# A transformer block's attention: probabilities transposed in quarters of 32 rows instead of halves of 64

## The chip, the cores and the metric

The kernel runs on one core of one Trainium2 chip. The metric is the device time of one execution in microseconds. Before the change it was 1009.75 us, the median of three runs (1009.56 to 1010.26).

## The reference

One layer of a diffusion backbone on 1024 latent tokens and 256 context tokens of width 1024, all in 32-bit floats. Half of the mixing width is a pooling mixer, half is neighbourhood attention with 8 heads of 64 on a latent grid of 16 rows by 64 columns; then come an output projection and a squared-ReLU MLP. The change lies in the attention. Cut to what matters:

```python
s_loc = einsum('bnqhd,brnkhd->bhnqrk', q_r, k_b) * scale       # 8 x 16 window
s_loc = where(col_mask, s_loc + bias, -inf)                    # learned 2-D bias
s_ctx = einsum('bnqhd,bkhd->bhnqk', q_r, k_ctx) * scale        # all context keys
p = softmax(concatenate([s_loc, s_ctx]), axis=-1)
o = einsum(p_loc, v_b) + einsum(p_ctx, v_ctx)
```

## The kernel before, in words

Whole kernel: a startup stage (modulation, norms, transposes of the tokens), the projections, the attention, the output projection and the MLP. All products are TensorE matmuls on 32-bit data, most of them on a split into a high and a low part. TensorE is busy nearly all the time.

The attention works through 32 *units* (`units`, L1232), a pair of heads `j` (0 to 3) by a tile `m` (0 to 7) of 128 queries, 16 grid rows by 8 columns. The two heads of a pair lie on partitions 0 to 63 and 64 to 127. An *inner* unit (m from 1 to 6) has 384 local keys and 256 context keys, 640 in all; a unit at the edge of the grid has 512. Each unit goes through these steps:

- `scores` (L1255): products of queries and keys for each of the heads e = 0, 1 into a pair of PSUM banks S. Weights are 64 rows (the head's features) by 128 queries; the two heads run side by side in the two halves of the array.
- `biased` (L1275): VectorE adds the table of bias and mask, writes the rows `sp` to SBUF and the row's extreme `nm`.
- `exps` (L1286): ScalarE takes the exponential in place and sums each row. `share` (L1290, L1292) makes the reciprocals of the sums and spreads them over `rb` of 128x128, on GpSimd.
- `turn` (L1298 to L1317): TensorE transposes the probabilities, so that the keys lie on the partitions. A transpose is a matmul with the block of probabilities as the weights and a piece of the identity as the streamed data. A block of 128 queries by 128 keys is turned in two halves of 64 queries, one in each half of the array, each into a bank of its own. The *side blocks* go to the columns of the banks `pa` and `pz`: the reciprocals, and for an inner unit the fifth block of keys of each head. The eight *main blocks* (four by two heads) go to the two banks `T_0` and `T_1`, 512 columns each.
- `fifth_kept` (L1322): ScalarE copies the side blocks to SBUF (`px`), a copy for each bank. `turn_kept` (L1327): ScalarE copies T_0 and VectorE T_1 into the page `pt`, 128x512 each.
- `values` (L1342): the value sums, 16 or 20 matmuls with weights of 128 keys by 64 features, the two heads in the two column halves of the array, into one of two places in `pa`, by turns.
- `weighed` (L1352): VectorE multiplies the sum with the turned reciprocals into the page `f`.

The loop over units (`for i in range(N)`) interleaves them by hand. In round i stand, in this order, `weighed(i-4)`, `scores(i)`, `biased(i)`, then what else the round has to do for other stages (`jobs`, loads, sums by DMA), `turn(i-2)`, its side copies, `exps(i, 0)`, the first copy of the turn, `exps(i, 1)`, the second copy, and `values(i-3)`. Each engine's queue keeps this order. Both T banks, and pa and pz, are there once: the turn of a round waits until the copies of the round before are done. The last two units (N-2 and N-1) are turned after the loop, between the first sums of the output projection; the last of them goes to a tile of its own, `Tlate`.

pa and pz also serve, in round 2, three small column sums (`mod_gate`, `column_sums`, matmuls at L264).

Of the kernel before, what the change touches and what calls it, by code (L numbers as in the profile page):

```python
# [11 lines left out]
F32 = mybir.dt.float32  # L12
# [6 lines left out]
P = 128  # L19
# [7 lines left out]
HD = 64  # L27
# [8 lines left out]
NM = GW // QC  # L36
# [72 lines left out]
def hybrid_block(ctx, tc, x, ctx_in, w_mod, mod_pages, w_u, b_mod, gp1, gp2, w_in, pool_w, rpb, w_out, w1, w2, vectors,  # L109
                 mask, edge, out):  # L110
    nc = tc.nc
# [15 lines left out]
    def page(name, dt=F32):  # L127
        return act.tile([P, 1024], dt, tag="pg", name=name)
# [21 lines left out]
    ident = cst("ident", [P, P])  # L150
# [123 lines left out]
    def mod_gate(name, acc, g, bank):  # L274
        nc.vector.tensor_tensor(acc[:, :256], mod_sums_of(name, acc, bank), g, mul)
# [23 lines left out]
    with tc.tile_pool(name="ps1", bufs=6, space=PSUM) as ps1, tc.tile_pool(name="tmp1", bufs=3) as tmp:  # L299

        def bank(name):
            if name[:2] == "pm" or name in ("pxt5", "pxb2", "pxb3", "pxb4", "pxb5", "pcs", "pcr"):
                return lasting(name)
            return ps1.tile([P, 512], F32, tag="mm", name=name)
# [9 lines left out]
        cols = cst("cols", [P, 56])  # L314
# [195 lines left out]
        whole, pt = {}, {}  # L510
# [320 lines left out]
        accs = {}  # L831
# [14 lines left out]
        def column_sums(name, acc, bank):  # L846
            nc.scalar.copy(acc[:, :256], mod_sums_of(name, acc, bank))
# [332 lines left out]
        with in_order(ET.PE, ET.Pool, ET.Activation, ET.DVE, ET.SP) as pooling:  # L1180
            banks = {of: [bank(f"p{of}{j}") for j in range(2)] for of in "KQ"}
            use(-1)
            for step, (n, of, j) in enumerate([(n, of, j) for n, of in products for j in range(2)]):
                half_product(n, of, j, banks[of])
                use(step)
                if step in (5, 9, 17):
                    name = {5: "S1", 9: "S4", 17: "S3"}[step]
# [4 lines left out]
                if step in (7, 11):  # L1192
                    name = {7: "S4", 11: "S3"}[step]
# [32 lines left out]
    with (  # L1226
# [9 lines left out]
        both_sides = {None: (pa[:, 256:448], pz[:, :192])}  # L1236


        def scores(i):
            j, m = units[i]  # L1240
# [54 lines left out]

        def turn(i, t=None, more=None):  # L1298
            inner = 0 < units[i][1] < NM - 1
            if t is None:  # L1300
                t = [bank(f"T{i}_{h}") for h in range(2)]
            sides = both_sides[i] = more or both_sides[None]
            turned[i] = t
            halves = [slice(h * HD, (h + 1) * HD) for h in range(2)]

            def both(to, src):
                for h, hs in enumerate(halves):
                    nc.tensor.transpose(to(h), src(hs), ident[hs, hs])  # L1308
# [9 lines left out]
        def fifth_kept(i):  # L1318
            n = (3 if 0 < units[i][1] < NM - 1 else 1) * HD
            fifths[i] = att.tile([P, 384], F32, tag="px", name=f"px{i}", bufs=4).rearrange("p (h t) -> p h t", h=2)  # L1320
            for h in range(2):
                nc.scalar.copy(fifths[i][:, h, :n], both_sides[i][h][:, :n])  # L1322

        def turn_kept(i, h, copy):
            if h == 0:
                turns[i] = page(f"pt{i}").rearrange("p (e i t) -> p e i t", e=2, i=4)
            copy(turns[i].rearrange("p e i t -> p (e i) t")[:, :, h * HD : (h + 1) * HD],  # L1327
                 turned[i][h].rearrange("p (a t) -> p a t", a=8))

        def values(i):  # L1330
            j, m = units[i]
            vc = [vcp[:, 0:512], vcp[:, 512:1024]]
            if 0 < m < NM - 1:
                vs = vb[m - 1 : m + 2] + vc
            else:
                o = 1 if m == 0 else 0
                vs = vc + vb[m + o - 1 : m + o + 1]
            cols = slice((i % 2) * P, (i % 2 + 1) * P)
            for c, v in enumerate(vs):
                for e in range(2):  # L1340
                    f = (2 * j + e) * HD
                    nc.tensor.matmul(pa[e * HD : (e + 1) * HD, cols], v[:, f : f + HD],  # L1342
                                     turns[i][:, e, c] if c < 4 else fifths[i][:, :, (e + 1) * HD : (e + 2) * HD],
                                     start=(c == 0), stop=(c == len(vs) - 1))


        def weighed(i):
            j, m = units[i]
            if m == 0:
                heads[j] = page(f"f{j}")  # L1350
            to = heads[j].rearrange("p (m h t) -> p m h t", h=2, t=HD)[:, m, ::-1, ::-1]
            nc.vector.tensor_tensor(to, pa[:, (i % 2) * P : (i % 2 + 1) * P].rearrange("p (h t) -> p h t", h=2),  # L1352
                                    fifths[i][:, :, :HD], mul)

        N = len(units)
# [88 lines left out]
        with in_order(ET.PE, ET.Activation, ET.DVE, ET.SP) as projected:  # L1444
# [16 lines left out]
            def right_added(j):  # L1461
# [16 lines left out]
            rest_of_bank = lambda name: pz[:, 256:]  # L1478
            for i in range(N):
                if i in LOADS:  # L1480
                    weight_load(0, kks[LOADS.index(i)])
                if i == N - 2:
                    G1 = gate_page("a")
                if i > 3:
                    weighed(i - 4)
                if i == 0:
                    gain = mod_gain(gp1, att.tile([P, 256], F32, tag="gp", name="gpa"), nc.sync)
                    accs["sh"] = page("accsh2")
                    nc.sync.dma_start(accs["sh"], kept_row)
                if i == 2:  # L1490
                    mod_gate("a", accs["a"], gain, rest_of_bank)
# [12 lines left out]
                for f, *args in jobs.get(i, ()):  # L1504
                    f(*args)
                if block_copies and (i < 4 or 6 < i):
                    block_copied()
                for _ in range(SUMS.count(i)):
                    block_summed()
                if i == 2:  # L1510
                    late_query = part_page("qP0_1", False)
                    qparts[0, 1] = late_query[:, :512], late_query[:, 512:]
                    high_part(qT[0][1], qparts[0, 1][0])
                if i > 1:
                    turn(i - 2)
                    fifth_kept(i - 2)
                if i == 2:
                    turn_kept(0, 0, nc.scalar.copy)
                    column_sums("sc", accs["sc"], lambda name: pa[:, :256])
                if i == N - 1:  # L1520
                    turn_kept(i - 2, 0, nc.scalar.copy)
                    turn_kept(i - 2, 1, nc.vector.tensor_copy)
                    biased(i, 1)
                exps(i, 0)
                if i == 2:
                    column_sums("sh", accs["sh"], rest_of_bank)
                if 2 < i < N - 1:
                    turn_kept(i - 2, 0, nc.scalar.copy)
                exps(i, 1)
                if i == 0:  # L1530
                    key_parts(2, 0, True, "lo")
                    key_parts(2, 1, True, "lo")
                    query_parts(2, 0, False, "lo")
                if 1 < i < N - 1:
                    turn_kept(i - 2, 1, nc.vector.tensor_copy)
# [30 lines left out]
            weighed(N - 3)  # L1566
            low()
            turn(N - 2)
            fifth_kept(N - 2)
            first_sums_kept(0)  # L1570
            late = ps_s.tile([P, 1024], F32, tag="S", name="Tlate")
            turn(N - 1, [late[:, :512], late[:, 512:]], (pa[:, 448:], pz[:, 448:]))
            turn_kept(N - 2, 0, nc.scalar.copy)
            turn_kept(N - 2, 1, nc.vector.tensor_copy)
            fifth_kept(N - 1)
            turn_kept(N - 1, 0, nc.scalar.copy)
            turn_kept(N - 1, 1, nc.vector.tensor_copy)
            weight_split(5)
            weight_split(6)
            first_sums(1)  # L1580
# [950 lines left out]
```

## Time and profile before

| | |
|---|---|
| median of three runs | 1009.75 us |
| the profiled execution's own time | 1010.35 us |
| its span, first to last instruction | 1008.6 us |
| granted TensorE clock | 0.998 of full speed |
| transposes of turns into T | 225.0 to 316.7 us of the span |
| TensorE busy from 255 to 270 us | 15.00 of 15.00 us |
| VectorE, ScalarE, GpSimd in the same stretch | 12.04, 13.54, 14.83 us |

The trace gives each instruction's start and duration. In the lists a group reads: line, engine, operation, tile written and tiles read, rows by columns of the array for a matmul, shape, count. PE stands for TensorE's matmuls, PEld for its weight loads, DVE for VectorE, ACT for ScalarE, POOL for GpSimd. A weight load of the next matmul can run while a matmul streams. Since a matmul's record includes its way through the array, records of successive ones overlap; the cost of one in a row of them is the distance between starts. In a timeline, successive equal instructions are merged to one row with the start of the first, the time to the end of the last, and their count.

### The profile page before, as it was taken

What the parts mean: (1) busy time and instruction counts of PE and PEld (TensorE: products, weight loads), DVE (VectorE), ACT (ScalarE), POOL (GpSimd) and SP (SyncE); (2) the same over time, 40 slices, a digit from 0 to 9 for tenths busy, and PEclk for the clock granted to TensorE, in tenths of its full rate; (3) what the DMA queues carried; (4) which work ended last, traced back from release to release, by engine and by line L of the source; (5) the groups of instructions that cost most, each with busy time, mean ns of one, the idle gap of its engine ahead of it and who ended that gap; (6) DMA issues with size and microseconds to landing.
All of it is one profiled execution on the core that took longest, in us unless ns stands there. A gap on an engine that the chain in (4) does not pass through costs nothing.

```text
span 1008.6 us, 16695 instructions
## 1 busy us (share of the span) xinstructions
PE 997.9 (99%) x6062; PEld 829.4 (82%) x6062; DVE 798.6 (79%) x1276; ACT 581.0 (58%) x1038; POOL 201.9 (20%) x278
## 2 busy tenths in 40 slices
PE   8999999999999999999999999999999999999997
PEld 5788888878998888888888888888888888888886
DVE  5589766968885689879998888754798888888895
ACT  6673254448886746786555544545556565544551
POOL 4111110166985232410000000000001000021121
PEclk9999999999999999999999999999999999999999
DMA  9999798665989979986776666625999999579944
GB/s 362 396 278 340 237 273 306 219 160 194 230 184 249 238 191 274 297 208 205 261 252 217 201 215 221 213 89 184 333 371 300 286 341 322 171 220 315 318 166 162
DMA packets 146882, 252.10 MB, mean 250 GB/s; under 512 B 10417, under 2 KB 76849, under 8 KB 146801
## 3 DMA queue, kind: packets, MB, share of 16 engines
q1 hardware_dynamic: 111024, 181.63, 52.9%
q0 software_dynamic: 18640, 38.45, 19.8%
q10 hardware_dynamic: 17136, 30.97, 8.3%
q8 instruction: 47, 0.77, 0.3%
q14 instruction: 35, 0.28, 0.1%
HBM read 197.52 MB, written 69.22 MB: 264 GB/s over the span
## 4 chain that ended last, share of the span: by engine, by line
PE 96%; DVE 1%; DMA 1%; ACT 1%; issue 0%; POOL 0%; SPq 0%; DVEq 0%; POOLq 0%; ACTq 0%
PE pu L481 5%; PE pyiM L2394 4%; PE pyiN L2394 4%; PE pa L1342 4%; PE S L1255 3%; PE phx L226 3%; PE phz L226 3%; PE phv L226 3%; PE pyx L226 3%; PE pyx L227 3%; PE pyx L228 3%; PE phx L228 3%; PE phz L228 3%; PE phv L228 3%; PE phx L227 3%; PE phv L227 3%
## 5 line engine op out<-in xcount | busy, mean ns | idle before, releaser
L1962 ACT ACTIVATE c<-c 128x512 f32<-128x512 f32 x48 | 30.3, 631 | 44.2 <-DVE c L2084 25.3
L174 ACT CAST wpS<-S 128x512 fp32r<-128x512 f32 x64 | 38.7, 617 | 28.6 <-PE phv L228 10.1
L1286 ACT ACTIVATE sp<-sp,nm 128x640 f32<-128x640 f32 (+1 forms) x64 | 51.4, 804 | 6.1 <-DVE ri L1290 5.0
L1275 DVE CUSTOM_DVE_ANT_0 sp<-S,tab 128x640 f32<-128x640 f32 (+1 forms) x56 | 44.5, 795 | 13.0 <-PE pz L1308 9.8
L226 PE MATMUL phx<-thB,wpA 128*128 128x512 f32 x128 | 50.2, 392 | 0.0
L180 DVE TENSOR_TENSOR wpS<-S,wpS 128x512 fp32r<-128x512 f32 x64 | 43.4, 686 | 8.2 <-ACT wpS L174 8.2
L228 PE MATMUL phx<-thB,wpA 128*128 128x512 f32 x128 | 49.8, 389 | 0.0
L227 PE MATMUL phx<-tlB,wpA 128*128 128x512 f32 x128 | 49.8, 389 | 0.0
L216 POOL DMA_DIRECT2D t<-in_w x16 | 19.3, 1207 | 105.8 <-PE pyx L228 31.8
L1963 ACT ACTIVATE c<-c 128x512 f32<-128x512 f32 x48 | 30.3, 630 | 15.8 <-DVE sa L2047 12.1
L243 POOL MEMSET accb<- 128x1024 f32 x1 | 1.0, 958 | 142.1 <-ACT c L1963 142.1
L226 PEld LDWEIGHTS phx<-thB,wpA 128*128 128x128 f32 x128 | 24.0, 188 | 5.4 <-ACT s L2015 0.4
L228 PEld LDWEIGHTS phx<-thB,wpA 128*128 128x128 f32 x128 | 24.0, 188 | 5.1
L227 PEld LDWEIGHTS phx<-tlB,wpA 128*128 128x128 f32 x128 | 24.0, 188 | 4.9
L1342 PE MATMUL pa<-pt,v 128*64 128x128 f32 x352 | 25.8, 279 | 0.0
L226 PE MATMUL phz<-thB,wpS 128*128 128x512 f32 x64 | 25.0, 391 | 0.0
L226 PE MATMUL phv<-thT,wpA 128*128 128x512 f32 x64 | 25.0, 391 | 0.0
L228 PE MATMUL phz<-thB,wpS 128*128 128x512 f32 x64 | 24.9, 389 | 0.0
L228 PE MATMUL phv<-thT,wpA 128*128 128x512 f32 x64 | 24.9, 389 | 0.0
L227 PE MATMUL phv<-tlT,wpA 128*128 128x512 f32 x64 | 24.9, 389 | 0.0
L226 PE MATMUL phy<-thT,wpS 128*128 128x512 f32 x64 | 24.9, 389 | 0.0
L227 PE MATMUL phy<-tlT,wpS 128*128 128x512 f32 x64 | 24.9, 389 | 0.0
(1191 smaller groups left out, 3568.8 us busy)
## 6 DMA issues: line engine op xcount, KB each, us to landing
hrA<-hdA SPq DMA_DIRECT2D x24, 512.0 KB, 7.3
wm<-in_mod_pages SPq DMA_DIRECT2D x16, 512.0 KB, 9.3
wa_0w<-in_w SPq DMA_DIRECT2D x16, 512.0 KB, 4.8
wa_1w<-in_w SPq DMA_DIRECT2D x16, 512.0 KB, 4.3
hdA<-c ACTq DMA_DIRECT2D x32, 256.0 KB, 2.3
hdS<-sa ACTq DMA_DIRECT2D x32, 256.0 KB, 3.0
hqS<-sb ACTq DMA_DIRECT2D x32, 256.0 KB, 3.9
b<-in_w SPq DMA_DIRECT2D x16, 512.0 KB, 8.3
```

Of the source, the lines that this page charges most:

```text
L174: nc.scalar.copy(hi, src)
L180: nc.vector.tensor_tensor(lo, src, hi.bitcast(F32), sub)
L226: nc.tensor.matmul(ps, ahi, bhi, start=first, stop=False, skip_group_check=more)
L227: nc.tensor.matmul(ps, ahi, blo, start=False, stop=False, skip_group_check=more)
L228: nc.tensor.matmul(ps, alo, bhi, start=False, stop=last, skip_group_check=more)
L481: nc.tensor.matmul(pus[b][j], wk(wgt, k, low, j * P, P), r, start=(k == 0 and n == 0), stop=(k == KT - 1 and n == 2))
L1275: nc.vector.tensor_tensor_reduce(out=to, in0=s, in1=bt, scale=1.0, scalar=BIG, op0=add, op1=ALU.min, accum_out=nm)
L1286: nc.scalar.activation(sp, sp, AF.Exp, bias=least[i, e], scale=-1.0, accum_out=sums[i][:, e : e + 1])
L1342: nc.tensor.matmul(pa[e * HD : (e + 1) * HD, cols], v[:, f : f + HD], turns[i][:, e, c] if c < 4 else fifths[i][:, :, (e + 1) * HD : (e + ...
L1962: nc.scalar.activation(r, src, AF.Relu)
L1963: nc.scalar.activation(r, r, AF.Square)
L2394: nc.tensor.matmul(to, a[part][:, j * 256 + t * P : j * 256 + (t + 1) * P], r, start=h + j == 0 and n < 2, stop=ends and n > 1)
```

## The change

The main blocks are turned in four quarters of 32 queries, each in its own quarter of the array's rows and into its own bank: the two banks of a new tile `pq`, which takes the place of `pa` and `pz`, and the two T banks. Each main block leaves 32 columns in each bank, so the eight blocks fill the first 256 columns of the four banks. The side blocks stay in halves of 64 queries, in the columns behind that in `pq`. A turn therefore has 32 main transposes where it had 16.

The copies follow the banks: `sides_kept` copies the side blocks of both banks in one ScalarE instruction, `pair_kept` the main columns of both pq banks in one ScalarE instruction (512 elements, as before), `banks_kept` the T banks in two VectorE instructions of 256 elements each where there was one of 512.

The value sums go to the free columns of a T bank (`weighed_sum`), so that the next turn, which writes those banks, also has to wait for `weighed` on VectorE. The small sums of round 2 move to free or not yet used columns. The last unit, `last_turn`, stays in halves of 64.

```diff
-        pa, pz = (ps_o.tile([P, 512], F32, tag=n, name=n) for n in ("pa", "pz"))
+        pq = ps_o.tile([P, 1024], F32, tag="pq", name="pq").rearrange("p (h x) -> p h x", h=2)
+        QUAD = P // 4
+        rest_of = lambda t: t[:, 8 * QUAD :]
+
+        def weighed_sum(i):
+            return rest_of(turned[i + 1][(i + 1) % 2] if i < N - 3 else turned[N - 3 + (i > N - 3)][i == N - 1])[:, :P]
...
-            both(lambda h: sides[h][:, :HD], lambda hs: shares[i][hs])
-            for e in range(2 if inner else 0):
-                both(lambda h: sides[h][:, (e + 1) * HD : (e + 2) * HD], lambda hs: probs[i, e][hs, 4 * P : 5 * P])
-            for c in range(4):
-                for e in range(2):
-                    o = (4 * e + c) * HD
-                    both(lambda h: t[h][:, o : o + HD], lambda hs: probs[i, e][hs, c * P : (c + 1) * P])
...
+        def parts_turned(places, n, src, at):
+            for r, to in enumerate(places):
+                qs = slice(r * n, (r + 1) * n)
+                nc.tensor.transpose(to[:, at : at + n], src(qs), ident[qs, qs], tile_position=(r * n, 0))
+
+        def turn(i):
+            t = turned[i] = [bank(f"T{i}_{h}") for h in range(2)]
+            for f, src in enumerate(side_blocks(i)):
+                parts_turned([pq[:, h] for h in range(2)], HD, src, 8 * QUAD + f * HD)
+            for b, src in enumerate(main_blocks(i)):
+                parts_turned([pq[:, 0], pq[:, 1], *t], QUAD, src, b * QUAD)
+
+        def sides_kept(i):
+            n = len(side_blocks(i)) * HD
             fifths[i] = att.tile([P, 384], F32, tag="px", name=f"px{i}", bufs=4).rearrange("p (h t) -> p h t", h=2)
+            nc.scalar.copy(fifths[i][:, :, :n], pq[:, :, 8 * QUAD : 8 * QUAD + n])
...
+        def pair_kept(i, copy):
+            copy(turn_page(i)[:, :, : 2 * QUAD].rearrange("p b (r t) -> p r b t", r=2),
+                 pq[:, :, : 8 * QUAD].rearrange("p r (b t) -> p r b t", b=8))
+
+        def banks_kept(i, copy):
             for h in range(2):
+                copy(turn_page(i)[:, :, (2 + h) * QUAD : (3 + h) * QUAD],
+                     turned[i][h][:, : 8 * QUAD].rearrange("p (b t) -> p b t", b=8))
...
-                    nc.tensor.matmul(pa[e * HD : (e + 1) * HD, cols], v[:, f : f + HD],
-                                     turns[i][:, e, c] if c < 4 else fifths[i][:, :, (e + 1) * HD : (e + 2) * HD],
+                    nc.tensor.matmul(to[e * HD : (e + 1) * HD], v[:, f : f + HD],
+                                     turns[i][:, 2 * c + e] if c < 4 else fifths[i][:, :, (e + 1) * HD : (e + 2) * HD],
```

In the loop, `sides_kept`, `pair_kept` and `banks_kept` stand where `fifth_kept` and the two calls of `turn_kept` stood.

How this moves the instructions, first on TensorE. Before, the turn of unit 9 begins so (rb is the page of reciprocals, sp the probabilities of a head, and the names end in a number of the buffer):

```order
L1308 MATMUL pa<-ident,rb_2853 128x64
L1308 MATMUL pz<-ident,rb_2853 128x64
L1308 MATMUL pa<-ident,sp_1_0_2779 128x64
L1308 MATMUL pz<-ident,sp_1_0_2779 128x64
L1308 MATMUL pa<-ident,sp_1_1_2786 128x64
L1308 MATMUL pz<-ident,sp_1_1_2786 128x64
L1308 MATMUL T_0_2929<-ident,sp_1_0_2779 128x64
L1308 MATMUL T_1_2930<-ident,sp_1_0_2779 128x64
```

Six side transposes are followed by 16 main ones, all of 64 streamed columns. The same place in the changed program:

```order
L1310 MATMUL pq<-ident,rb_2980 128x64 x2
L1310 MATMUL pq<-ident,sp_1_0_2890 128x64 x2
L1310 MATMUL pq<-ident,sp_1_1_2897 128x64 x2
L1310 MATMUL pq<-ident,sp_1_0_2890 128x32 x2
L1310 MATMUL T_0_3072<-ident,sp_1_0_2890 128x32
L1310 MATMUL T_1_3073<-ident,sp_1_0_2890 128x32
L1310 MATMUL pq<-ident,sp_1_1_2897 128x32 x2
L1310 MATMUL T_0_3072<-ident,sp_1_1_2897 128x32
```

The side transposes stand as they did; from the fourth row on each block has four instructions of 32 streamed columns, by turns into the two banks of pq and T_0 and T_1.

On VectorE, the end of round 20 and the head of round 21 before the change (pt is the page of the turned probabilities, f that of the results, px the side blocks, ISA the pass of `biased`):

```order
L1327 COPY pt_3605<-T_1_3577 128x8x64
L1352 TENSOR_TENSOR f_3544<-pa,px_3525 128x128
L1275 ISA sp_5_0_3634,nm_0_3635<-S_5_0_3620,tab_1993 128x640
L1275 ISA nm_0_3635 128x1
L1290 RECIPROCAL ri_3637<-su_3603 128x2
```

And the same place (the head of round 21) in the changed program:

```order
L1335 COPY pt_3907<-T_0_3863 128x8x32
L1335 COPY pt_3907<-T_1_3864 128x8x32
L1371 TENSOR_TENSOR f_3831<-T_0_3863,px_3812 128x128
L1278 ISA sp_5_0_3937,nm_0_3938<-S_5_0_3923,tab_1993 128x640
L1278 ISA nm_0_3938 128x1
```

The copy has become two, and the product that follows reads a T bank in place of pa; the order around them is the same.

More of the change, by code (lines that the diff above doesn't have):

```diff
@@ L1294, in share, with side_blocks @@
                 ri.rearrange("p (e o) -> p e o", o=1).to_broadcast([P, 2, HD]))
-        def turn(i, t=None, more=None):
+        def side_blocks(i):
             inner = 0 < units[i][1] < NM - 1
[L1300 to L1308, printed above, removed]
-            both(lambda h: sides[h][:, :HD], lambda hs: shares[i][hs])
-            for e in range(2 if inner else 0):
-                both(lambda h: sides[h][:, (e + 1) * HD : (e + 2) * HD], lambda hs: probs[i, e][hs, 4 * P : 5 * P])
-            for c in range(4):
-                for e in range(2):
-                    o = (4 * e + c) * HD
-                    both(lambda h: t[h][:, o : o + HD], lambda hs: probs[i, e][hs, c * P : (c + 1) * P])
@@ L1318, in fifth_kept @@
-        def fifth_kept(i):
-            n = (3 if 0 < units[i][1] < NM - 1 else 1) * HD
-            fifths[i] = att.tile([P, 384], F32, tag="px", name=f"px{i}", bufs=4).rearrange("p (h t) -> p h t", h=2)
-            for h in range(2):
[L1322 to L1328, printed above, removed]
+            return [lambda hs: shares[i][hs]] + [lambda hs, e=e: probs[i, e][hs, 4 * P : 5 * P] for e in range(2 * inner)]
@@ new lines, in hybrid_block @@
+        main_blocks = lambda i: [lambda qs, e=e, c=c: probs[i, e][qs, c * P : (c + 1) * P] for c in range(4) for e in range(2)]
+        def parts_turned(places, n, src, at):
[8 more added lines that the diff above has]
+                parts_turned([pq[:, 0], pq[:, 1], *t], QUAD, src, b * QUAD)
@@ new lines, in sides_kept, with turn_page @@
+        def sides_kept(i):
+            n = len(side_blocks(i)) * HD
+            fifths[i] = att.tile([P, 384], F32, tag="px", name=f"px{i}", bufs=4).rearrange("p (h t) -> p h t", h=2)
+            nc.scalar.copy(fifths[i][:, :, :n], pq[:, :, 8 * QUAD : 8 * QUAD + n])
+        def turn_page(i):
+            if i not in turns:
+                turns[i] = page(f"pt{i}").rearrange("p (b q) -> p b q", b=8)
+            return turns[i]
+        def pair_kept(i, copy):
+            copy(turn_page(i)[:, :, : 2 * QUAD].rearrange("p b (r t) -> p r b t", r=2),
+                 pq[:, :, : 8 * QUAD].rearrange("p r (b t) -> p r b t", b=8))
@@ new lines, in banks_kept, with last_turn, last_kept @@
+        def banks_kept(i, copy):
+            for h in range(2):
+                copy(turn_page(i)[:, :, (2 + h) * QUAD : (3 + h) * QUAD],
+                     turned[i][h][:, : 8 * QUAD].rearrange("p (b t) -> p b t", b=8))
+        def last_turn(i, late, sides):
+            parts_turned(sides, HD, side_blocks(i)[0], 0)
+            for b, src in enumerate(main_blocks(i)):
+                parts_turned(late, HD, src, b * HD)
+        def last_kept(i, late):
+            fifths[i] = att.tile([P, 384], F32, tag="px", name=f"px{i}", bufs=4).rearrange("p (h t) -> p h t", h=2)
+            nc.scalar.copy(fifths[i][:, :, :HD], pq[:, :, 512 - HD :])
+            for h, copy in enumerate((nc.scalar.copy, nc.vector.tensor_copy)):
+                copy(turn_page(i)[:, :, h * HD : (h + 1) * HD], late[h].rearrange("p (b t) -> p b t", b=8))
@@ L1337, in values @@
                 vs = vc + vb[m + o - 1 : m + o + 1]
-            cols = slice((i % 2) * P, (i % 2 + 1) * P)
+            to = weighed_sum(i)
             for c, v in enumerate(vs):
@@ L1351, in weighed @@
             to = heads[j].rearrange("p (m h t) -> p m h t", h=2, t=HD)[:, m, ::-1, ::-1]
-            nc.vector.tensor_tensor(to, pa[:, (i % 2) * P : (i % 2 + 1) * P].rearrange("p (h t) -> p h t", h=2),
+            nc.vector.tensor_tensor(to, weighed_sum(i).rearrange("p (h t) -> p h t", h=2),
                                     fifths[i][:, :, :HD], mul)
@@ L1477, in hybrid_block @@
                     29: [(weight_split, 2, True)], 30: [(weight_split, 3, True)]}
-            rest_of_bank = lambda name: pz[:, 256:]
             for i in range(N):
@@ L1490, in hybrid_block @@
                 if i == 2:
-                    mod_gate("a", accs["a"], gain, rest_of_bank)
+                    mod_gate("a", accs["a"], gain, lambda name: pq[:, 1])
                 if i in (5, 6):
@@ L1515, in hybrid_block @@
                     turn(i - 2)
-                    fifth_kept(i - 2)
+                    sides_kept(i - 2)
                 if i == 2:
-                    turn_kept(0, 0, nc.scalar.copy)
-                    column_sums("sc", accs["sc"], lambda name: pa[:, :256])
+                    pair_kept(0, nc.scalar.copy)
+                    column_sums("sc", accs["sc"], lambda name: rest_of(turned[0][0]))
                 if i == N - 1:
-                    turn_kept(i - 2, 0, nc.scalar.copy)
-                    turn_kept(i - 2, 1, nc.vector.tensor_copy)
+                    pair_kept(i - 2, nc.scalar.copy)
+                    banks_kept(i - 2, nc.vector.tensor_copy)
                     biased(i, 1)
@@ L1525, in hybrid_block @@
                 if i == 2:
-                    column_sums("sh", accs["sh"], rest_of_bank)
+                    column_sums("sh", accs["sh"], lambda name: rest_of(turned[0][1]))
                 if 2 < i < N - 1:
-                    turn_kept(i - 2, 0, nc.scalar.copy)
+                    pair_kept(i - 2, nc.scalar.copy)
                 exps(i, 1)
@@ L1534, in hybrid_block @@
                 if 1 < i < N - 1:
-                    turn_kept(i - 2, 1, nc.vector.tensor_copy)
+                    banks_kept(i - 2, nc.vector.tensor_copy)
                 if i == 2:
@@ L1568, in hybrid_block @@
             turn(N - 2)
-            fifth_kept(N - 2)
+            sides_kept(N - 2)
             first_sums_kept(0)
             late = ps_s.tile([P, 1024], F32, tag="S", name="Tlate")
[L1572 to L1577, printed above, removed]
+            late_of = [late[:, :512], late[:, 512:]], [pq[:, h, 512 - HD :] for h in range(2)]
+            last_turn(N - 1, *late_of)
+            pair_kept(N - 2, nc.scalar.copy)
+            banks_kept(N - 2, nc.vector.tensor_copy)
+            last_kept(N - 1, late_of[0])
             weight_split(5)
```

1 line of the change is left out of this document (removed).

## Prediction

> **What bounds the kernel now.** I read the page of the profile first, then the chain of waits and the waits of the attention stage (about 224 to 317 us of the span), then one unit of it instruction by instruction.
>
> ```profile
> span 1008.6 us, 16695 instructions
> PE 997.9 (99%) x6062; PEld 829.4 (82%) x6062; DVE 798.6 (79%) x1276; ACT 581.0 (58%) x1038; POOL 201.9 (20%) x278
> PE 96%; DVE 1%; DMA 1%; ACT 1%; issue 0%; POOL 0%; SPq 0%; DVEq 0%; POOLq 0%; ACTq 0%
> ```
>
> The third line is the chain that ended last: 96% of it is TensorE, so what the change does to TensorE's time in the attention stage comes out at the end of the kernel nearly undiminished. The busy figure itself says little, since a matmul's record includes its way through the array. What counts is the distance from one start to the next. Here is a turn, the step that is changed, with the scores ahead of it and the value sums behind it, in TensorE's timeline (start, time to the last end, line, tile, count):
>
> ```profile
> 263.33 0.28 PE L1255 MATMUL S<-kP1h,qP 64*128 64x256 f32 x2
> 263.45 0.21 PE L1308 MATMUL pa<-ident,rb 64*128 64x64 f32 x1
> 263.50 0.22 PE L1308 MATMUL pa<-ident,sp 64*128 64x64 f32 x1
> 263.57 0.22 PE L1308 MATMUL pa<-ident,sp 64*128 64x64 f32 x1
> 263.63 0.67 PE L1308 MATMUL T<-ident,sp 64*128 64x64 f32 x16
> 264.23 0.88 PE L1342 MATMUL pa<-pt,v 128*64 128x128 f32 x12
> ```
>
> Pairs of half transposes start about 0.06 us apart. The sixteen main ones (eight pairs) take 0.67 - 0.22 = 0.45 us from first to last start, so the last starts at 264.08, and a pair costs 0.45 / 7 = 0.064 us; the chain's own row gives 0.50 / 8 = 0.0625, which I use:
>
> ```profile
> 263.80 0.50 PE T L1308 x16
> 264.30 1.24 PE pa L1342 x20
> ```
>
> **What sets those 0.0625 us?** Either the data that streams through the array (64 columns) or the weights that are loaded for each block (128 columns). The weight loads of the same turn:
>
> ```profile
> 263.45 0.14 PEld L1308 LDWEIGHTS pa<-ident,sp 64*128 64x128 f32 x1
> 263.51 0.14 PEld L1308 LDWEIGHTS pa<-ident,sp 64*128 64x128 f32 x1
> 263.57 0.59 PEld L1308 LDWEIGHTS T<-ident,sp 64*128 64x128 f32 x16
> ```
>
> Each matmul starts 0.05 to 0.06 us after the load of its own weights began (263.45 to 263.50, 263.51 to 263.57, 263.57 to 263.63), and the next load into the same rows begins within 0.01 us of that start. Load, start, load, start: the period is a load and a handover. The streaming comes to less. These are durations (minimum/median/maximum, in ns) of the transposes, and of the whole 128-row transposes at the head of the kernel:
>
> ```profile
> L1308 PEld LDWEIGHTS T<-ident,sp x496: 135/139/143, 225.0 to 316.7; 64*128 64x128 f32 x166
> L1308 PE MATMUL T<-ident,sp x496: 221/223/226, 225.0 to 316.7; 64*128 64x64 f32 x166
> L377 PEld LDWEIGHTS pxt<-ident,x x32: 137/141/226, 8.6 to 19.4; 128*128 128x128 f32 x32
> L377 PE MATMUL pxt<-ident,x x32: 271/272/332, 8.6 to 19.5; 128*128 128x128 f32 x32
> ```
>
> From 64 to 128 streamed columns a matmul grows by 272 - 223 = 49 ns, so 64 columns stream in about 49 ns and 32 in about 25. The load of 128 columns takes 139 ns with 64 rows and 141 with 128: its time doesn't hang on the rows.
>
> **The change part by part.** Main blocks: eight pairs of 64 rows become eight groups of four of 32 rows, each half as long in streamed columns, with weights of 128 columns as before. If rows don't matter to a load, a group of four costs what a pair does, 0.0625 us, provided four loads run beside each other as two do now. What the halved stream saves is hidden under the load. Call the cost of a group P; its bounds come below.
>
> Change of shape. Before, all 22 transposes of a turn have the shape of the scores ahead of them (64 rows by 128 columns), as the order in the section on the change shows. Now the side blocks keep it and the main ones have 32 rows by 128, so the shape of the array's tiles changes within the turn. What such a change costs is in the trace: from the last transpose to the value sums, 264.08 to 264.23, is 0.15 us. And, into a turn behind whole matmuls, near the end of the stage:
>
> ```profile
> 315.50 0.39 PE L227 MATMUL pox<-wo_1l,mix 128*128 128x512 f32 x1
> ...
> 315.73 0.39 PE L228 MATMUL pox<-wo_1h,mix 128*128 128x512 f32 x1
> 316.05 0.27 PE L1308 MATMUL pa<-ident,rb 64*128 64x64 f32 x1
> ...
> 316.16 0.22 PE L1308 MATMUL pa<-ident,sp 64*128 64x64 f32 x1
> ```
>
> 0.32 us where 0.23 is the rule, and then a first interval of 0.11 in place of 0.06, because the first load isn't hidden. Without a change of shape (scores to turn, 263.33 to 263.45) there is none of this. No row shows 64 rows followed by 32; I take it to cost what the change behind the same 64-column transposes costs, 0.15 and then 0.11; the other end is nothing (0.0625 twice). The Trainium skill, TensorEngine Tiling (Array Packing), section Tiling Modes, says that a change of tiling mode drains the engine; the trace agrees wherever the shape changes, with 0.15 to 0.32 us. By this rule a unit loses what is summed up next; without it a unit would gain a little, which is a rival below.
>
> The sum for a unit, from the first side pair to the value sums. Before: 10 x 0.0625 + 0.15 = 0.775 (the rows give 264.23 - 263.45 = 0.78). After: two side intervals 0.125, the change of shape 0.15, the first group 0.11, six more 6P, and from the last group to the value sums 0.15 - 0.025 = 0.125 since its stream is 25 ns shorter: 0.51 + 6P. With P = 0.0625 that is 0.885, so **0.11 us more for each unit**. It is the same where a unit has one side block, for only side intervals drop out, on both sides. 31 of the 32 units are turned so; the last keeps 64 rows but now follows groups of 32, a further change of shape, of which I count 0.05, since it has waits of its own. 31 x 0.11 + 0.05 = 3.5 us.
>
> Even P = 0.044 would only break even. That is the point of this change: it has to earn a drain before it earns anything.
>
> The copies. VectorE's copy of one bank (128x512) becomes two of 128x256, ScalarE's two side copies become one.
>
> ```profile
> L1327 DVE COPY pt<-T 128x512 f32<-128x512 f32 x31 | 21.3, 686 | 1.6 <-PE T L1308 1.6
> L275 DVE TENSOR_TENSOR acca<-pz,gpa 128x256 f32<-128x256 f32 x1 | 0.4, 418 | 0.0
> L1322 ACT COPY px<-pa 128x192 f32<-128x192 f32 x24 | 7.6, 315 | 4.2 <-PE pz L1308 3.4 <-PE pa L1308 0.3
> L1327 ACT COPY pt<-T 128x512 f32<-128x512 f32 x31 | 17.6, 569 | 0.2 <-PE T L1308 0.2
> ```
>
> VectorE: 2 x 418 - 686 = 150 ns more per unit. ScalarE: 569 ns for 512 against 315 for 192 is 0.79 ns an element, so 384 in one take about 470 where two took about 630: 160 ns less. Its other copy keeps 512 elements. Neither reaches the path, as the timeline of both engines in one unit shows:
>
> ```profile
> 258.64 0.80 DVE L1275 CUSTOM_DVE_ANT_0 sp<-S,tab 128x640 f32<-128x640 f32 x1
> ...
> 259.37 0.69 DVE L1327 COPY pt<-T 128x512 f32<-128x512 f32 x1
> ...
> 259.63 0.44 PE L1255 MATMUL S<-kP1h,qP 64*128 64x384 f32 x2
> ...
> 259.97 0.28 DVE L1352 TENSOR_TENSOR f<-pa,px 128x128 f32<-128x128 f32 x1
> ...
> 260.61 0.21 PE L1308 MATMUL pa<-ident,rb 64*128 64x64 f32 x1
> ...
> 260.81 0.82 DVE L1275 CUSTOM_DVE_ANT_0 sp<-S,tab 128x640 f32<-128x640 f32 x1 [0.56 <-PE pz L1308]
> ```
>
> VectorE idles 0.56 us in a unit until the next scores are there; 0.15 more fits in.
>
> The moved sums. The value sums leave pa for the free half of a T bank, so the next turn's groups wait in T for the product that reads them (the row at 259.97, over at 260.25; with 0.15 more ahead of it, 260.40). The turn begins at 260.61 and its groups two side intervals and a change of shape later, at 260.61 + 0.125 + 0.15 = 260.89. The cover is 0.49 us; I cost it at nothing. If it went, TensorE would stand with all that follows in its queue, the value sums and the next scores.
>
> **The rivals.**
>
> *The groups run faster than a load (faster or even).* If four loads of 32 rows overlapped more than two do, the stream would set P: 25 ns and the same 10 ns of handover, 0.035. Then 0.51 + 0.21 = 0.72, 0.055 less a unit, 1.7 us in all: 1008.0. Without the handover, P = 0.027, it is 3.2 less: 1006.5. Against it stands that loads are no shorter for half the rows. Chance 0.14, half of it beyond 0.2%.
>
> *No drain between 64 and 32 rows.* With P = 0.0625 a unit then saves only the last group's 25 ns: 0.8 us, 1009.0. Chance 0.08. With groups of 0.035 as well, a unit takes 3 x 0.0625 + 7 x 0.035 + 0.125 = 0.56 and would save 0.22, of which VectorE lets 0.19 pass: its second pass over the scores ends at 258.64 + 0.80 = 259.44 and the next scores, in the same banks, start at 259.63. 31 x 0.19 = 5.9 us, 1003.9. Chance 0.04.
>
> *The supply of instructions becomes the bound (slower by more).* A group holds eight instructions where a pair held four. The densest long run of small matmuls in the trace is this one, four side by side, of 32 columns:
>
> ```profile
> 11.78 1.08 PE L415 MATMUL pm<-wm,sT 128*32 128x128 f32 x32
> ```
>
> (1.08 - 0.27) / 31 = 0.026 us from start to start; four of them 0.105. If no run of matmuls could be denser, P = 0.105, the unit comes to 0.51 + 0.63 = 1.14, 0.365 more, 11.3 us: 1021.1. It decides from P = 0.0625, where eight instructions no longer fit into a load. Against it: the two halves of a pair start 0.01 us or less apart now, so short bursts are denser, and the L415 run is explained by its own stream of 128 columns. The Trainium skill, TensorE: Matmul & The Clock Gate, Part 1, gives about 25 ns from start to start as the floor however few columns a matmul has; by that P would be 0.10 and the time about 1020. No run here has so few columns in such a row, and the trace neither bears it out nor refutes it. Chance 0.13, with values of P in between.
>
> *A wait on T (slower).* Should the product that frees T come more than 0.49 us later than I read, each unit loses what exceeds it; with 0.1 us on top of the drain 31 x 0.21 = 6.5, 1016.3. Chance 0.04.
>
> **How the numbers follow.** The profiled execution took 1010.35 us, 1008.6 of them its span; it is 0.6 above the median of 1009.75, and no term depends on that, so the 3.5 us are added to the median: 1013.2. This case has the remaining 0.57. Its own range, with P from 0.060 to 0.070 and some of the added time swallowed by waits in the first units, is 1012.4 to 1014.7. For the range I leave out the fast groups below P = 0.035 and the case without drain and load (0.11 together), and most of the supply rival (0.09): from 1007.9 to 1016.5, where the upper end is P = 0.080 (0.51 + 0.48 = 0.99, 0.215 more, 6.7 us). About 0.2% (2 us) is what a measurement of this kernel can tell from no change. Faster than that: half of the first rival, the combined case and a little for a saving that I don't see, 0.13. Within it: the other half, no drain, and a forecast that the later stages swallow, 0.20. Slower: 0.67.
>
> **What would show it.** Right: in the timeline the last 64-row side transpose and the first 32-row one stand 0.15 us apart, the next 0.11, the rest of the groups 0.06, the weight loads of 32 rows still take about 139 ns, and a turn from first side block to value sums takes 0.885 us. VectorE's idle time ahead of the score pass falls by the 0.15 of its second copy and grows by the longer turn. Wrong: groups 0.035 apart or 0.10 apart, no gap at the change of shape, or TensorE's weight loads waiting for VectorE's product at T.

## The result, and the profile after

The changed kernel takes 1067.56 us (median of four runs, 1065.04 to 1072.06) against 1009.71 (1009.56 to 1010.26): slower by a factor of 1.0577, 95% interval 1.0538 to 1.0615, or 58 us. The direction was forecast; the size was 3.5 us. Its profiled execution took 1065.04 us, the fastest of the four; its span is 54.7 us longer than before, and that is what I take apart here.

From the page of the changed kernel: the span, busy times, TensorE's busy tenths and granted clock in 40 slices, and the engines of the chain that ended last.

```profile
span 1063.3 us, 17622 instructions
PE 1012.9 (95%) x6558; PEld 840.6 (79%) x6558; DVE 802.5 (75%) x1307; ACT 577.3 (54%) x1006; POOL 202.2 (19%) x278
...
PE   8999999987777799999999999999999999999997
...
PEclk9999999999979999999999999999999999999999
...
PE 90%; DVE 5%; issue 2%; DMA 2%; ACT 1%; SPq 0%; DVEq 0%; ACTq 0%
```

TensorE's row of before:

```profile
PE   8999999999999999999999999999999999999997
```

VectorE's share of the chain went from 1% to 5%. In five slices in a row, 239 to 372 us, TensorE is now busy seven tenths, and they lie in the attention stage. Who waits there? The waits of the attention stage (engine, line, releaser: us in total, times, longest), L1361 being the value sums, L1335 VectorE's copies of the T banks, L1322 the copy of the side blocks, L1371 `weighed`:

```profile
ACT px L1322 <- PE T L1310: 67.9, 30, 3.8
...
PEld T L1361 <- DVE pt L1335: 42.2, 29, 2.2
DVE f L1371 <- PE T L1361: 39.0, 30, 2.2
PE T L1361 <- DVE pt L1335: 38.9, 29, 2.1
```

The second row is the find: in 29 units of 32 the value sums wait for `banks_kept`, 42.2 us in all. Two of the other rows are engines that wait for TensorE, and the fourth is the second again, seen from the matmuls. One unit in the timeline (start, time to the last end, engine, line, what it does, count, idle time before it and releaser):

```profile
240.47 0.88 PE L1361 MATMUL T<-pt,v 128*64 128x128 f32 x12 [1.59 <-DVE pt L1335]
...
241.71 0.44 PE L1258 MATMUL S<-kP0h,qP 64*128 64x384 f32 x2
...
242.71 0.22 PE L1310 MATMUL pq<-ident,rb 64*128 64x64 f32 x2
...
242.77 0.47 PE L1310 MATMUL pq<-ident,sp 64*128 64x64 f32 x6
242.91 0.82 DVE L1278 CUSTOM_DVE_ANT_0 sp<-S,tab 128x640 f32<-128x640 f32 x1 [0.79 <-PE pq L1310]
...
242.99 0.25 PE L1310 MATMUL T<-ident,sp 32*128 32x32 f32 x2
...
243.07 0.23 PE L1310 MATMUL pq<-ident,sp 32*128 32x32 f32 x2
...
243.44 0.23 PE L1310 MATMUL pq<-ident,sp 32*128 32x32 f32 x2
...
243.74 0.80 DVE L1278 CUSTOM_DVE_ANT_0 sp<-S,tab 128x640 f32<-128x640 f32 x1
...
244.47 0.75 DVE L1335 COPY pt<-T 128x256 f32<-128x256 f32 x2
...
244.94 0.88 PE L1361 MATMUL T<-pt,v 128*64 128x128 f32 x12 [1.26 <-DVE pt L1335]
```

Read it as a loop. The next scores stand behind the value sums on TensorE and start 1.24 us after them (240.47 to 241.71). VectorE's first pass over these scores starts 1.20 us later (242.91). The copies stand on VectorE behind both passes, 1.56 us later (244.47). The first of the two takes 0.42, and 0.05 after its end the sums start that go to its bank (244.94). 1.24 + 1.20 + 1.56 + 0.42 + 0.05 = 4.47 us, where a unit of this kind took 3.00 before (258.39 to 261.39, in the rows of before that follow). Where the sums' bank is the second one copied, a unit takes about 0.35 more; where VectorE's passes cover an edge unit, less.

Before, the sums went into pa, and what had to leave pa first was the side blocks, which ScalarE copies early. The timeline of before at the same place shows how near that was:

```profile
257.99 0.32 ACT L1322 COPY px<-pa 128x192 f32<-128x192 f32 x1
...
258.39 0.88 PE L1342 MATMUL pa<-pt,v 128*64 128x128 f32 x12
...
261.39 0.88 PE L1342 MATMUL pa<-pt,v 128*64 128x128 f32 x12
```

The copy ends at 258.31, the sums start at 258.39: the same kind of wait, covered by 0.08 us, of which the 0.05 from a copy's end to the start of what waits for it is needed. The order of the two programs with their waits shows the exchange, first before, then after; in brackets stands the semaphore waited for, named by the engine that raises it:

```
L1342 MATMUL pa<-pt_3679,v_1180 64x128 [waits Activation_49]
L1361 MATMUL T_0_4040<-pt_3997,v_1180 64x128 [waits DVE_49]
```

It is not their data that the sums wait for. They read pt_3997, the page of their own unit, which was filled a round earlier; the copy in front of them empties T_0_4040, the bank that they write, and fills the page of the next unit (in the loop, `banks_kept(i-2)` stands ahead of `values(i-3)`).

Why do sums in columns 256 and up wait for a copy of columns 0 to 255? The program guards the bank, not the columns. The Trainium skill, PSUM — Partial Sum Buffer, section "PSUM bank collisions raise a hardware error", says that two engines must not reach the same bank and the same quadrant of 32 partitions at once, whatever the columns. Every kernel here keeps that wait, so no run shows what would happen without it.

What else is in the 54.7 us? Nearly all of them fall into the attention stage: the transposes into T run from 225.3 to 371.0 us, which is 54.0 longer than from 225.0 to 316.7. The turn itself, first side pair to last group, takes 243.44 - 242.71 = 0.73 us where before took 0.63. And the granted clock fell in parts of the stage, each time to half of full speed. These are the stretches (length, busy PE, PEld, DVE, ACT, POOL, then the clock as a share, the DMA share, GB/s; edges rounded to 0.1 us):

```profile
263.80:270.70 6.90, 5.83 (x72) 5.25 (x72) 2.77 (x9) 2.59 (x6) 3.81 (x6) 0.51 0.39 60
301.40:315.00 13.60, 11.78 (x144) 10.62 (x146) 5.49 (x17) 5.18 (x12) 6.06 (x12) 0.50 0.62 117
318.50:321.90 3.40, 3.40 (x32) 3.07 (x28) 0.39 (x2) 0.46 (x2) 0.87 (x3) 0.50 0.00 0
345.80:349.20 3.40, 3.18 (x24) 2.85 (x26) 0.46 (x2) 1.25 (x3) 2.40 (x3) 0.50 0.79 134
```

They make 27.3 us; before, the clock of the stage is full. What that costs can be had from the four runs: at a mean clock of 0.987 the kernel took 1065.04 us, at 0.977 it took 1072.06, and the other two lie between. So 0.010 of clock, 21 us at half speed, cost 7 us, and 27.3 us cost about 9. The estimate for the span: 42 (waits) + 3.3 (31 turns at 0.105, between the 0.10 of these rows and the 0.11 of experiment 3) + 9 (clock) = 54. A small part of the 42, the gap that stood between turn and sums before too, counts too much in it; in experiment 2, 39 us of such waits are worth 36.

### The profile page after: what moved, and what is told of

The parts are those of the page before. It is cut to its first block, busy times and chain, and to the rows that moved or that the text cites. A ratio compares the mean times of both kernels' runs of the same rounds, so it can differ in the third digit from the quotient of the medians.

```text
span 1063.3 us, 17622 instructions
## 1 busy us (share of the span) xinstructions
PE 1012.9 (95%) x6558; PEld 840.6 (79%) x6558; DVE 802.5 (75%) x1307; ACT 577.3 (54%) x1006; POOL 202.2 (19%) x278
## 4 chain that ended last, share of the span: by engine, by line
PE 90%; DVE 5%; issue 2%; DMA 2%; ACT 1%; SPq 0%; DVEq 0%; ACTq 0%
PE T L1361 4%; PE pu L481 4%; PE pyiM L2411 4%; PE pyiN L2411 4%; PE S L1258 3%; PE phx L226 3%; PE phv L226 3%; PE phz L226 3%; PE pyx L226 3%; PE pyx L227 3%; PE phv L228 3%; PE phz L228 3%; PE pyx L228 3%; PE phx L227 3%; PE phx L228 3%; PE phz L227 3%
## 5 line engine op out<-in xcount | busy, mean ns | idle before, releaser
L1361 PE MATMUL T<-pt,v 128*64 128x128 f32 x352 | 28.1, 296 | 28.9 <-DVE pt L1335 28.9
L1322 ACT COPY px<-pq 128x384 f32<-128x384 f32 (+1 forms) x31 | 13.3, 430 | 71.5 <-PE T L1310 67.9
L1361 PEld LDWEIGHTS T<-pt,v 128*64 128x64 f32 x352 | 20.8, 146 | 31.7 <-DVE pt L1335 31.4
L1371 DVE TENSOR_TENSOR f<-T,px 128x128 f32<-128x128 f32 x32 | 9.3, 291 | 39.1 <-PE T L1361 39.0
L1310 PE MATMUL pq<-ident,sp 32*128 32x32 f32 (+1 forms) x592 | 28.4, 232 | 0.0
L1310 PEld LDWEIGHTS pq<-ident,sp 32*128 32x128 f32 (+1 forms) x592 | 24.5, 146 | 2.5
L1361 PE MATMUL T<-pt,vc 128*64 128x128 f32 x160 | 16.4, 307 | 10.0 <-DVE pt L1335 10.0
L1335 DVE COPY pt<-T 128x256 f32<-128x256 f32 x62 | 23.4, 417 | 3.3 <-PE T L1310 2.4
```

The costliest lines, as they stand in the source:

```text
L1310: nc.tensor.transpose(to[:, at : at + n], src(qs), ident[qs, qs], tile_position=(r * n, 0))
L1361: nc.tensor.matmul(to[e * HD : (e + 1) * HD], v[:, f : f + HD], turns[i][:, 2 * c + e] if c < 4 else fifths[i][:, :, (e + 1) * HD : (e + 2 ...
```

## The experiments

Theory 1: the value sums in a T bank wait for VectorE's copies, which stand behind two passes over scores that come after the sums before. Theory 2: the narrow transposes cost the time, by their number or their shape. Theory 3: the side copy, now one instruction for both banks of one tile, waits for the whole turn (67.9 us of waits above) and delays what follows. The kernel before ran beside the experiments, with medians of 1010.35 us in the first four and 1010.44 in the last four.

**1. Halves in place of quarters, sums still in T (`rows64`).** Edit, on the changed kernel: the main blocks are turned 64 rows at a time again, four blocks into pq and four into T; the copies follow.

```diff
-                parts_turned([pq[:, 0], pq[:, 1], *t], QUAD, src, b * QUAD)
+                parts_turned([pq[:, 0], pq[:, 1]] if b < 4 else t, HD, src, b % 4 * HD)
...
```

> The changed kernel with one thing undone: the main blocks are turned in halves of 64 rows again, four blocks into the two banks of pq and four into the two T banks, so that banks, copies and sums stay as the change left them. Theory 1 (the value sums wait because VectorE has yet to copy the bank that they now share): the turn lies beside VectorE's passes and is off the path, so the time stays that of the changed kernel, 1063 to 1072 us, and the wait ahead of the value sums stays at 1.2 to 1.9 us or grows by the 0.1 us that the turn gets shorter. Theory 2 (transposes of 32 rows are what costs): the time falls back to about 1010 us.

Measured: 1059.54 us (1057.23 to 1063.37), 1.0479 times before, interval 1.0462 to 1.0497. Its waits:

```profile
PEld T L1361 <- DVE pt L1335: 47.5, 29, 2.5
```

Not one transpose of 32 rows is left in the loop, and 49 of the 58 us are still there. Theory 2 falls as the main cause. The wait has grown by 5 us: of the same loop a turn that is 0.11 us shorter leaves more to wait for, 29 x 0.11 = 3 us of the 5. The time lies below the 1063 to 1072 that I expected. Its clock was higher, 0.990 to 0.995 in its four runs against 0.977 to 0.987, and by the reckoning above 0.010 of clock are worth 7 us.

**2. The wait alone, put into the kernel before (`late_side`).** Edit, on the kernel before: VectorE, not ScalarE, copies the side blocks out of pa, ahead of its copy of T and so behind its two passes. Layout, transposes and places of the sums stay.

```diff
-                nc.scalar.copy(fifths[i][:, h, :n], both_sides[i][h][:, :n])
+                if h == 1 or not 0 < i < N - 3:
+                    nc.scalar.copy(fifths[i][:, h, :n], both_sides[i][h][:, :n])
...
+            nc.vector.tensor_copy(fifths[i][:, 0, :n], both_sides[i][0][:, :n])
...
+                if 2 < i < N - 1:
+                    side_kept_late(i - 2)
```

The third added line is the body of `side_kept_late`, which is called ahead of VectorE's `turn_kept`.

> The kernel before, transposes of 64 rows and all, with one copy moved: the side blocks in pa, the bank that the value sums are written to, are copied by VectorE behind its two passes over the scores, not by ScalarE right behind the side transposes. Theory 1 (a wait for a copy out of the same bank): value sums start about 4.4 us apart (1.24 from value sums to scores, 1.20 to VectorE's first pass, 1.56 for the passes, 0.35 for the copy, 0.05 for the signal), 1.4 to 1.5 more than now for 27 units, 40 us, and some more if the clock falls: 1048 to 1060 us. Theory 2 (32 rows): there are none here, so within 2 us of 1010.

Measured: 1046.28 us (1046.11 to 1046.54), 1.0356, interval 1.034 to 1.0371. Waits, then a unit of the timeline (L1347 are the sums, L1327 the copy):

```profile
PEld pa L1347 <- DVE px L1327: 39.2, 28, 1.5
```

```profile
263.49 0.35 DVE L1327 COPY px<-pa 128x192 f32<-128x192 f32 x1
...
263.90 0.66 PE L1347 MATMUL pa<-pt,vc 128*64 128x128 f32 x8 [1.32 <-DVE px L1327]
...
267.67 0.35 DVE L1327 COPY px<-pa 128x192 f32<-128x192 f32 x1
...
268.08 0.66 PE L1347 MATMUL pa<-pt,v 128*64 128x128 f32 x8 [1.32 <-DVE px L1327]
```

One copy moved behind the passes, 3.83 us from copy end to copy start and 4.18 us for a unit: the loop of the changed kernel, made in the old one. Its 36 us lie just under my range: the units are shorter than the 4.4 us that I reckoned with, and the clock stays full (0.999).

**3. The T banks copied early (`scalar_T`, `scalar_T_64`).** Edit, on the changed kernel: ScalarE and VectorE trade copies. ScalarE takes the T banks, right behind the turn and the sums' bank first; VectorE takes the pair in pq, which no sums share. `scalar_T_64` adds the edits of the first experiment.

```diff
-            for h in range(2):
+            for h in (i % 2, 1 - i % 2):
...
+                    banks_kept(i - 2, nc.scalar.copy)
...
-                    pair_kept(i - 2, nc.scalar.copy)
...
-                    banks_kept(i - 2, nc.vector.tensor_copy)
+                    pair_kept(i - 2, nc.vector.tensor_copy)
```

> The changed kernel with the copies of the two pairs of banks exchanged: ScalarE copies the T banks right behind the turn, the one that takes the next value sums first, and VectorE copies pq behind its passes. Theory 1: the value sums wait for a copy of 0.37 us and two signals behind the turn in place of VectorE's passes, about 0.55 us over the 0.15 of a change of shape; with the 0.11 of the turn itself 0.65 us a unit, 20 us: 1026 to 1034 us, with the clock at full speed. Theory 2 (32 rows): stays above 1060 us.

> The kernel with the exchanged copies and, besides, the main blocks in halves of 64 rows in the same four banks. Here the turn lies on the path, so the difference to the exchanged copies with 32 rows is what 32 rows cost by themselves. By the prediction's term (a change of shape within the turn, groups no faster than pairs) 0.11 us a unit: 3.4 us less than with 32 rows. If groups of 32 rows were cheaper than pairs by more than the change of shape costs, this one would be slower.

Measured: 1032.0 us (1031.22 to 1033.99), 1.0217, interval 1.0202 to 1.0233; and 1026.21 (1026.16 to 1026.64), 1.0158, interval 1.0143 to 1.0173. The waits of the first, and TensorE around a turn of each:

```profile
PEld T L1361 <- ACT pt L1335: 18.7, 29, 0.7
```

```profile
260.52 0.22 PE L1310 MATMUL pq<-ident,rb 64*128 64x64 f32 x2
...
261.26 0.22 PE L1310 MATMUL T<-ident,sp 32*128 32x32 f32 x1
...
261.98 0.33 PE L1361 MATMUL T<-pt,v 128*64 128x128 f32 x2 [0.49 <-ACT pt L1335]
```

```profile
259.08 0.21 PE L1310 MATMUL pq<-ident,rb 64*128 64x64 f32 x2
...
259.52 0.41 PE L1310 MATMUL T<-ident,sp 64*128 64x64 f32 x8
260.39 0.88 PE L1361 MATMUL T<-pt,v 128*64 128x128 f32 x12 [0.46 <-ACT pt L1335]
```

Same bank, same columns, an earlier copy by another engine: 36 of the 58 us are gone. What is left is the copy itself, which must follow the turn: about half a microsecond, not covered. The pair also measures the narrow transposes under an equal wait. The turn takes 261.26 - 260.52 = 0.74 us against 259.52 + 0.41 - 0.22 - 259.08 = 0.63, so 0.11 more, and the wait is 0.03 to 0.04 longer: 31 x 0.15 = 4.65 us. The difference of the medians is 5.8 where I expected 3.4. Of the remaining microsecond, `scalar_T` shows one idle stretch of 1.15 us that its profile puts to no releaser, which I can't explain.

**4. VectorE's copies between its two passes (`T_first`).** Edit, on the changed kernel: the second pass moves behind the copies.

```diff
-                if i < N - 1:
+                if i < 3:
                     biased(i, 1)
...
+                if 2 < i < N - 1:
+                    banks_kept(i - 2, nc.vector.tensor_copy)
+                    biased(i, 1)
...
-                if 1 < i < N - 1:
+                if i == 2:
                     banks_kept(i - 2, nc.vector.tensor_copy)
```

> The changed kernel with VectorE's copies of the T banks put between its two passes over the scores, not behind them. Theory 1 (value sums wait for these copies): they come 0.8 us earlier, so value sums start 3.7 to 4.1 us apart and the time falls by about 23 us: 1036 to 1046. Theory 2 (32 rows): no change, 1063 to 1072. That ScalarE's side copy now waits for the whole turn (theory 3): no change either.

Measured: 1040.03 us (1039.67 to 1040.74), 1.0295, interval 1.028 to 1.031.

```profile
ACT px L1322 <- PE T L1310: 41.3, 30, 3.8
...
PEld T L1361 <- DVE pt L1335: 25.4, 29, 1.5
```

TensorE's wait fell from 42.2 to 25.4 us by the order of VectorE alone. The side copy still waits for the whole turn, and the time came out where theory 1 has it: theory 3 falls.

**5. The sums always in the bank that is copied first (`sums_T0`).** Edit, on the changed kernel:

```diff
-            return rest_of(turned[i + 1][(i + 1) % 2] if i < N - 3 else ...
+            return rest_of(turned[i + 1][i == N - 4] if i < N - 3 else ...
```

> The changed kernel with the value sums always in the first T bank, which VectorE copies first, not in the two by turns. Theory 1: the units that waited for the second copy wait 0.33 us less, half of 31 units, 5 us: about 1061. Theories 2 and 3: 1063 to 1072, no difference.

Measured: 1055.41 us (1054.48 to 1057.85), 1.045, interval 1.0435 to 1.0466.

```profile
PEld T L1361 <- DVE pt L1335: 39.2, 29, 1.9
```

3 us of wait are gone and 12 us of time, where I expected 5. Between the profiled executions of the two it is 10.6 us. `sums_T0` has 6.8 us at half clock in the stage, not 27.3; by the reckoning above that is 7 us, and 3 + 7 make most of the 10.6. Why the clock fell less is not shown.

**6. Two changes of shape, and nothing else (`odd_shape`).** Edit, on the kernel before: one more transpose, of 32 rows, between side and main blocks, into columns of pa that nothing reads.

```diff
+            if i < N - 2: nc.tensor.transpose(pa[:, 448:480], ident[:32], ident[:32, :32], tile_position=(0, 0))
```

> The kernel before with a single transpose of 32 rows put between the side blocks and the main blocks of each turn (its result isn't used). Nothing else moves. If every change of tile shape costs 0.15 us and exposes the next load, and 32 streamed columns cost what 64 do, a unit takes 0.15 + 0.15 + 0.05 - 0.06 = 0.29 us more, 30 units, 8.6 us: about 1018. If 64 to 32 rows is no such change, within 3 us of 1010.

Measured: 1018.35 us (1018.18 to 1018.39), 1.008, interval 1.0063 to 1.0097.

```profile
266.49 0.22 PE L1308 MATMUL pa<-ident,sp 64*128 64x64 f32 x1
...
266.65 0.24 PE L1314 MATMUL pa<-ident 32*128 32x32 f32 x1
266.82 0.72 PE L1308 MATMUL T<-ident,sp 64*128 64x64 f32 x16
```

0.16 us into the shape of 32 rows and 0.17 out of it, where 0.06 would stand: 0.27 a unit, 30 units, 8.1 us; measured are 7.9. This is the price that the prediction took from other shapes, and a single small matmul pays it.

**7. How thin the cover was before (`sides_last`).** Edit, on the kernel before: the side blocks are turned behind the main ones, so their copy comes later.

```diff
-            both(lambda h: sides[h][:, :HD], lambda hs: shares[i][hs])
...
             for c in range(4):
...
+            both(lambda h: sides[h][:, :HD], lambda hs: shares[i][hs])
...
```

> The kernel before with the side blocks turned behind the main blocks. ScalarE's side copies then wait for the whole turn, as in the changed kernel, and pa, which takes the value sums, is copied that much later. Theory 1 (same bank): the value sums wait for the copy out of pa, about 0.22 + 0.05 + 0.32 + 0.05 = 0.64 us behind the last transpose in place of 0.15: 0.5 us a unit, 15 us, about 1025. Without a wait for the shared bank (theory 2) ScalarE has the slack: within 2 us of 1010.

Measured: 1022.51 us (1022.31 to 1023.05), 1.0122, interval 1.0107 to 1.0137.

```profile
PEld pa L1342 <- ACT px L1322: 15.1, 29, 0.5
```

The order of work within the turn alone turns the cover of 0.08 us into a wait of half a microsecond in 29 units; the time grows by 12 us. No product, copy or place differs.

## Why the prediction was wrong, point by point

- **Groups at the price of pairs, 0.0625 us.** Right. From 243.07 to 243.44 there are six intervals, 0.062 each. Neither the rival on the supply of instructions nor the one on faster groups took place. The floor of 25 ns a matmul that I quoted from the Trainium skill, TensorE: Matmul & The Clock Gate, Part 1, doesn't hold for four quarters side by side: four matmuls in 62 ns are 16 ns each. I had called the trace of before neutral on it, and it was not: there the two halves of a pair start some 0.01 us apart.
- **Change of shape, 0.15 and then 0.11.** Right for the first: two pairs of sides start at 242.77 and 0.06 later, the first group at 242.99, so 0.16; `odd_shape` has the same. The interval behind it is 0.08 (242.99 to 243.07), not 0.11.
- **25 ns less from the last group to the sums.** Wrong: 32 streamed columns last as long as 64. The T view of the changed kernel (minimum/median/maximum in ns) against the 221/223/226 of before:

```profile
L1310 PEld LDWEIGHTS T<-ident,sp x496: 132/138/224, 225.3 to 370.9; 32*128 32x128 f32 x166
L1310 PE MATMUL T<-ident,sp x496: 221/222/312, 225.3 to 371.0; 32*128 32x32 f32 x166
```

  The 25 ns came from comparing two matmuls that differ in the rows of the array too (64 and 128), not in the streamed columns alone. The misses, 0.03 too much behind the change of shape and 0.025 too little here, cancel by luck: about 0.105 us a unit, 3.3 us, where 3.5 were forecast. The Trainium skill, TensorEngine Tiling (Array Packing), section Instruction Overhead, has it that a matmul with one column takes as long as one with 60; the rows agree from 32 to 64.
- **The copies.** Near in their lengths: VectorE's two take 0.75 us together where I had 2 x 0.418 = 0.84, ScalarE's side copy 0.48 where I had 0.47. Wrong that none reaches the path: VectorE's is on it.
- **The moved sums.** This is the step that failed. It said: "The value sums leave pa for the free half of a T bank, so the next turn's groups wait in T for the product that reads them [...] The cover is 0.49 us; I cost it at nothing." That asks who waits for the reader of the sums. It doesn't ask what the sums themselves wait for: a bank has to be free of its former readers before they are written. The former reader had been ScalarE's early copy, and it became VectorE's late one. The price is 42 us of waits. The clock fell along with them and is full again with the shorter waits of `scalar_T`, but it is full in `late_side` too, with 39 us of waits; so how the clock's 9 us hang on this step is not settled by these runs. The rival "A wait on T" had the place, with the wrong waiter (the groups of the turn, not the value sums), the wrong thing waited for (the product, not the copies) and a price of 1016.3. What I said would show it wrong, TensorE waiting for VectorE at T, is what the profile shows, for `banks_kept` in place of the product.
- **The clock.** Not foreseen. A falling clock was no term and no rival.

The order of the changed program was enough to see the step: the sums' wait turns from ScalarE to VectorE in it, and in VectorE's rows the copies stand behind both passes. The trace of before had the times for it, from the sums to the next scores, to the pass, to the copy.

## What to carry to other kernels

Where a result moves to another bank, list what has to leave that bank first, on which engine and behind what it is queued there; columns that don't overlap were no protection in these programs. Follow that wait once around the loop, for a copy that stands behind work on the next step's data closes a circle that no engine's busy share shows. And look for how thin the cover of the old place was: here it was 0.08 us, and a later copy (`late_side`) or a later turn of the side blocks (`sides_last`) was enough to break it.

## What the runs showed that I had not expected

- **The clock falls under waits that are short.** No wait of the value sums in the changed kernel exceeds 2.2 us, yet TensorE ran at half speed for 27.3 us of the stage, in stretches of 3.4 us or a multiple of it. The Trainium skill, TensorE: Matmul & The Clock Gate, Part 1, gives half clock after an idle window of about 3.4 us; here shorter waits, repeated every 4.5 us, go with it. The longest wait of the sums and the time at half clock in the stage, in the profiled runs: 2.5 us with 20.5 (`rows64`), 2.2 with 27.3 (the changed kernel), 1.9 with 6.8 (`sums_T0`), 1.5 with 3.4 (`T_first`), 1.5 with none (`late_side`), 0.7 with none (`scalar_T`). That is a loose correlation in six kernels, and at half clock a wait may itself grow longer. The idle share of a stretch doesn't decide it alone: in `rows64` TensorE is busy for 1.69 us from 240.90 to 244.30, and the clock stays full; in `sums_T0` it is busy for more, 2.06 us from 253.10 to 256.50, and half clock follows. No run varied the idle time alone, so what decides stays open.
- **Half the rows don't shorten a weight load, and 32 streamed columns take a matmul as long as 64.** 138 ns for 32 rows against 139 for 64, and 222 ns for 32 columns against 223 for 64. A transpose cut into four narrow pieces therefore costs as much as one cut into two, and the shape must be changed for it.
